# A hybrid RWKV and convolution block: four of seven products side by side through the channels, and half of the weight sums on VectorE

## The chip, the cores and the metric

The kernel runs on one core of one Trainium2 chip. The metric is the device time of one execution in microseconds. Five engines work side by side, each in the order of its own queue: TensorE (PE in the profile, PEld for its weight loads), VectorE (DVE), ScalarE (ACT), GpSimd (POOL) and SyncE (SP), which here only issues DMA transfers. GpSimd issues transfers too, those that add what they bring to what is there.

## The reference, cut to what matters

One layer over 16 meta tokens and 512 tokens of width 2048: a norm, one input projection, a recurrence with a state per head (group A, 1024 channels), a gated convolution (group B, 1024 channels), one output projection, the residual, and a last norm. The change touches the output projection and the little before it:

```python
        y_b = Bg * _causal_depthwise_conv(Cg * hc, conv_w[l]) * jax.nn.silu(g_c)

        mix = jnp.concatenate([y_a, y_b], axis=-1)
        h_res = h_res + mix @ w_out[l]

    out = _rmsnorm(h_res, norm_f_g)
    return out[:, N_META:]
```

`mix` is 512 x 2048, `w_out` 2048 x 2048, all in float32.

## The kernel before

**The input part.** Tiles of 128 columns of the input projection run through TensorE one after the other (`main`, `steps`), from a generator `flow`; the matmuls of the recurrence are put between them. All other work is laid beside this stream. The last tiles are the four of the convolution for channel tile 7: C, h, B, gc. `use` turns the projection of gc into a mix tile `cv` (VectorE, L417), which is written to DRAM (`mixd`, L418) and read back into `mix3` by `split_mix` (L1045), as for all tiles of group B.

**Two parts of a number.** Each float32 operand is split in two parts of TensorE's faster float32 form: ScalarE casts the high part (`hi`, tiles `oh`, `wh`, L1155 and L124), VectorE subtracts it from the whole and gets the low part (`lo`, tiles `ol`, `wl`, L1156 and L125; some low parts of the input projection on GpSimd). A product of two such operands takes three matmuls: high by high, high by low, low by high. `hi` and `lo` have six buffers each; a block of 128 x 1024 weights is two such quarters, so the splits can be three blocks ahead of TensorE. Blocks arrive in `raw`, three buffers.

**The output projection** uses seven products of quarter matrices instead of eight (Strassen's way, in Winograd's form). `mix` is cut in two halves of tokens (T0, T1) and two halves of channels; `w_out` in halves of channels and, for each half of the 2048 output columns (`half` 0 and 1), two column blocks of 512. The left operands are quarters of `mix` or the sums S1, S3, S4, S5 of such quarters, made by `sums` (L1057 to L1060, once for each half `q` of the channel tiles) and split by `split_form` (L1096, L1097). The right operands are weight quarters or sums of them. A weight quarter is four blocks `g` of 256 channels; the block (k, col, g) of a half is `w_out[2 * half + col, 4 * k + g]`, 512 KB.

The products of one half come in this order: M1, M2, M7, Q6, P5, P4, M3, each with its four blocks g in a row. One product with one block is a unit: 12 matmuls of 512 columns (two token tiles s, two quarters, three matmuls; L1184). A product keeps two PSUM banks through its four units and is closed when they are done (`close`): VectorE adds it to the residual rows `xa` (columns 0 to 1023) or `xb` (1024 to 2047) (`onto`, L1165), or to the shared part `sh` (L1206, L1210), which GpSimd then adds to several places (L1207 after Q6, one operation for each s; L1212 after P5, two for each s). ScalarE sums squares of what is complete (`squares`, L1171), GpSimd multiplies by the gain of the last norm (`gain`, L1175).

The right operands of M7, Q6, P5 and P4 are weight sums. They are made by transfer: a block is loaded by SP into a chain tile `x` (M7, L1124), into `spare` or into a `raw` tile `wo` (P5, L1130, L1136), and GpSimd issues a transfer that adds another block to it (`add`, L1145, `accum_op=ALU.add`). Each of these four products has one such accumulation for every block: 16 in a half, 32 in all. M1, M2 and M3 take their blocks straight. The first two blocks of M1 are fetched with the stream of the input weights (`stream += [w_out[0, g] for g in range(2)]`).

`at(u, ...)` and the loop over `units` write down when a load, an accumulation or a split is issued, some units ahead. The order within TensorE is that of the program; on VectorE, ScalarE and GpSimd a scheduler with priorities sets it, up to the last section, where it is written by hand: the last product for the last half (M3 here) is done for token tile 0, then for tile 1 in two parts, while finished rows go out (`finish`, `finish_last`).

Of the kernel before, what the change touches and what calls it, by code (L numbers as in the profile page):

```python
# [18 lines left out]
P = 128  # L19
# [57 lines left out]
def hymba_kernel(ctx: ExitStack, tc: tile.TileContext, xt, xtok, w_in, w_out, pv, lup, cst, msk, gf, out):  # L77
# [39 lines left out]
    stream += [w_out[0, g] for g in range(2)]  # L117
# [257 lines left out]
    def use(what, i, ps):  # L375
# [31 lines left out]
        elif what == "B":  # L407
            cv = got["h", i]
            b = tm(f"b{i}")[:, 0:SEQ]
            scaled(REAL, ps, b, META)  # L410
            nc.gpsimd.tensor_tensor(out=cv, in0=cv, in1=b, op=ALU.mult)
        else:
            cv = got["h", i]
            g = tm(f"gc{i}")[:, 0:SEQ]
            scaled(REAL, ps, g, META)
            gate(g, f"c{i}")
            nc.vector.scalar_tensor_tensor(out=cv, in0=cv, scalar=0.5, in1=g, op0=ALU.mult, op1=ALU.mult)  # L417
            later(9000, lambda: nc.sync.dma_start(mixd[8 + i], cv))  # L418
        ready.add((what, i))

    ready = set()

# [596 lines left out]
    mix = [pp.tile([P, 4, SEQ], F32, tag=f"R{m}", name=f"mix{m}") for m in range(4)]  # L1019
    pt = ExitStack()  # L1020
# [5 lines left out]
    def split_mix(j):  # L1026
# [17 lines left out]
        else:  # L1044
# [30 lines left out]
    for _ in flow:  # L1075
        pass
    sums(1)
# [6 lines left out]
    xa = [pw.tile([P, 1024], F32, name=f"xa{t}") for t in range(4)]  # L1084
# [4 lines left out]
        for f in forms for q in range(2)  # L1089
    }  # L1090

# [11 lines left out]
    slot, right, chain = {}, {}, {}  # L1103
    spare = [None]
# [13 lines left out]
    def request(u):  # L1118
        half, prod, g = units[u]
        if prod in ("M1", "M2", "M3"):  # L1120
            k, c = {"M1": (0, 0), "M2": (1, 0), "M3": (1, 1)}[prod]
        elif prod == "M7":
            slot[u] = chain[g] = pw.tile([P, 1024], F32, tag=f"X{g}", name=f"x{half}{g}")
            nc.sync.dma_start(slot[u], rows_of(half, 0, 1, g))  # L1124
            return
        elif prod == "P5":
            k, c = 0, 0
            if g < 2:
                slot[u] = spare[0][:, 1024 * g : 1024 * g + 1024]
                nc.sync.dma_start(slot[u], rows_of(half, k, c, g))  # L1130
                return
        else:
            slot[u] = chain[g]
            return
        slot[u] = wp.tile([P, 1024], F32, tag="raw", name=f"wo{u}", bufs=3)
        nc.sync.dma_start(slot[u], rows_of(half, k, c, g))  # L1136


    ADDED = {"M7": (1, 1), "Q6": (0, 0), "P5": (0, 1), "P4": (1, 0)}

    def add(u):
        half, prod, g = units[u]
# [4 lines left out]
    def split_unit(u, home=None):  # L1147
        for q in range(2):
            rq = slot[u][:, q * 512 : (q + 1) * 512]
            if home is None:  # L1150
                hi = wp.tile([P, 512], F32R, tag="hi", name=f"oh{u}{q}", bufs=6)
                lo = wp.tile([P, 512], F32R, tag="lo", name=f"ol{u}{q}", bufs=6)
            else:
                hi, lo = home[q]
            nc.scalar.copy(hi, rq)  # L1155
            nc.vector.tensor_tensor(out=lo, in0=rq, in1=hi.bitcast(F32), op=ALU.subtract)  # L1156
            right[u, q] = (hi, lo)
# [9 lines left out]
    def squares(t, n, part=None):  # L1167
        o = slice(0, 512) if part is None else slice(256 * part, 256 * part + 256)
        sq = pw.tile([P, 512], F32, tag="sqj", name=f"sqj{n}_{t}_{part}")
        j = n + (part or 0)  # L1170
# [6 lines left out]
    def product(u, bank, s_):  # L1177
        half, prod, g = units[u]
        for s in s_:
            for q in range(2):  # L1180
                jj = 2 * g + q
                hi, lo = right[u, q]
                for n, (m, w) in enumerate(((0, hi), (0, lo), (1, hi))):
                    nc.tensor.matmul(  # L1184
                        bank[s], left(prod, jj, m, s), w, start=(jj == 0 and n == 0), stop=(jj == 7 and n == 2)
                    )


    def close(half, prod, z):
# [3 lines left out]
        for s in range(2):  # L1193
            d, p = shared[s], z[s]
# [3 lines left out]
            elif prod == "M2":  # L1198
                onto(s, n, p, ALU.add)
                squares(s, n)  # L1200
            elif prod == "M7":
                onto(2 + s, n + 1, p, ALU.subtract)
                onto(2 + s, n, p, ALU.add)
            elif prod == "Q6":
                with ahead():
                    nc.vector.tensor_tensor(out=d, in0=d, in1=p, op=ALU.add)  # L1206
                nc.gpsimd.tensor_tensor(out=here(2 + s, n), in0=here(2 + s, n), in1=d, op=ALU.add)  # L1207
            elif prod == "P5":
                with ahead():
                    nc.vector.tensor_tensor(out=d, in0=d, in1=p, op=ALU.add)  # L1210
                for t in (2 + s, s):
                    nc.gpsimd.tensor_tensor(out=here(t, n + 1), in0=here(t, n + 1), in1=d, op=ALU.subtract)  # L1212
                squares(2 + s, n + 1)
            elif prod == "P4":
                onto(2 + s, n, p, ALU.add)
                squares(2 + s, n)
            else:
                onto(s, n + 1, p, ALU.subtract)
                squares(s, n + 1)

    shared = []
    U = {(half, prod): 28 * half + 4 * PRODUCTS.index(prod) for half in range(2) for prod in PRODUCTS}
# [8 lines left out]
    xb = []  # L1231
# [6 lines left out]
    def load_gain():  # L1238
        t = pp.tile([P, 4, 512], F32, tag="R0", name="gfb").rearrange("p a b -> p (a b)")
        nc.sync.dma_start(t, gf.partition_broadcast(P))  # L1240
        return t

    def load_spare():
        spare[0] = pp.tile([P, 4, 512], F32, tag="R1", name="spare").rearrange("p a b -> p (a b)")

    N_FIRST = 2
    for u, (half, prod, g) in enumerate(units):
        if prod == "M3" and half:
            continue
        if u >= N_FIRST:  # L1250
            early = {"M7": 7, "P5": 5}.get(prod, 3)
            at(u - early, request, u)
            at(u - (4 if prod == "M7" else 3), add, u)
            at(u - 2, split_unit, u)
    for f, (prod, off) in {"S3": ("M1", 0), "S5": ("M2", 0), "S1": ("M7", 0), "S4": ("Q6", 0)}.items():
        for q in range(2):
            at(U[0, prod] + off + 2 * q, split_form, f, q)
    for t in range(4):
        at((-1, 0, 3, 4)[t], load_xa, t)
    at(U[0, "M7"] + 1, load_spare)  # L1260
    at(U[0, "P5"] + 1, lambda: globals_.update(gfb=load_gain()))
    for m in range(2):
        at(U[0, "P4"] + 2 + m, load_xb, m)
    globals_ = {}

    home = []

    def load_home(g):
        u = U[1, "M3"] + g
        request(u)  # L1270
        tiles = [
            pw.tile([P, 4, HT], F32R, tag=f"{f}{g % 2}{a}", name=f"home{g}{a}").rearrange("p a b -> p (a b)")
            for f in (("S3", "S5")[g // 2],) for a in range(2)
        ]
        split_unit(u, [(tiles[0][:, 512 * q : 512 * q + 512], tiles[1][:, 512 * q : 512 * q + 512]) for q in range(2)])

    for g in range(4):
        at(U[1, "P5"] + 1 + 2 * g, load_home, g)

    for q in range(2 * N_FIRST):  # L1280
        j = N_IN + q // 2
        right[q // 2, q % 2] = quarters[2 * j + q % 2]
    for fn, args in calls.pop(-1):
        fn(*args)
    gfb = None
    for u, (half, prod, g) in enumerate(units):
        if half and prod == "M3":
            break
        for fn, args in calls.pop(u, ()):
            fn(*args)  # L1290
        gfb = globals_.get("gfb")
        if g == 0:
            z = [po.tile([P, 512], F32, tag="o", name=f"{prod}{half}{s}") for s in range(2)]
# [143 lines left out]
```

## Time and profile before

| | us |
|---|---|
| median of three runs | 1065.77 (1063.74 to 1068.25) |
| the profiled execution, its time | 1065.86 |
| the profiled execution, its span | 1064.1 |
| granted TensorE clock, mean of the span | 0.984 |
| first matmul of the output projection starts | 860.64 |
| last matmul ends | 1055.23 |

Times in the profile are microseconds from the span's start, where not marked ns. In a group a row reads: line, engine, operation, output<-inputs, shapes and count; then busy time and the mean ns of one; then idle time of the engine before them and what ended most of it. In the table by stretches each engine has its busy time and in brackets its count of instructions; PEclk is the granted clock, the DMA share the mean busy share of the 16 DMA engines. In a table of waits the figures are total, times and longest. In a timeline a row is start, length, engine, line, operation.

### The profile page before, as it was taken

What the parts mean: (1) busy time and instruction counts of PE and PEld (TensorE: products, weight loads), DVE (VectorE), ACT (ScalarE), POOL (GpSimd) and SP (SyncE); (2) the same over time, 40 slices, a digit from 0 to 9 for tenths busy, and PEclk for the clock granted to TensorE, in tenths of its full rate; (3) what the DMA queues carried; (4) which work ended last, traced back from release to release, by engine and by line L of the source; (5) the groups of instructions that cost most, each with busy time, mean ns of one, the idle gap of its engine ahead of it and who ended that gap; (6) DMA issues with size and microseconds to landing.
All of it is one profiled execution on the core that took longest, in us unless ns stands there. A gap on an engine that the chain in (4) does not pass through costs nothing. (4 is left out here: it accounts for less than half of the span.)

```text
span 1064.1 us, 23777 instructions
## 1 busy us (share of the span) xinstructions
PE 1022.3 (96%) x9725; PEld 926.4 (87%) x9725; DVE 664.6 (62%) x1195; ACT 394.4 (37%) x726; POOL 313.2 (29%) x332
## 2 busy tenths in 40 slices
PE   8999999999999999999999999999999998759996
PEld 6999998999989999979999989898898985648875
DVE  6787765668653767653786652354556966567763
ACT  7544322434323444223433232222223353325543
POOL 0132323323222323222232222223323322262333
PEclk9999999999999999999999999999999999889999
DMA  8437386373754375743466649686736869998944
GB/s 293 135 108 167 90 208 184 102 175 106 190 165 126 109 167 119 185 139 103 128 145 164 181 116 329 196 262 182 226 97 178 252 231 291 258 268 243 208 99 159
DMA packets 190077, 188.45 MB, mean 177 GB/s; under 512 B 122128, under 2 KB 144400, under 8 KB 189584
## 3 DMA queue, kind: packets, MB, share of 16 engines
q1 hardware_dynamic: 184784, 169.09, 55.4%
q0 software_dynamic: 4608, 16.78, 8.1%
q8 instruction: 76, 1.25, 0.5%
q10 hardware_dynamic: 576, 1.07, 0.3%
q14 instruction: 33, 0.27, 0.1%
HBM read 150.02 MB, written 36.88 MB: 176 GB/s over the span
## 5 line engine op out<-in xcount | busy, mean ns | idle before, releaser
L125 POOL TENSOR_TENSOR wl<-wr,wh 128x512 fp32r<-128x512 f32 x123 | 171.1, 1391 | 377.0 <-ACT wh L124 354.2
L124 ACT CAST wh<-wr 128x512 fp32r<-128x512 f32 x258 | 156.3, 618 | 311.5 <-PE ps_k L313 52.0
L125 DVE TENSOR_TENSOR wl<-wr,wh 128x512 fp32r<-128x512 f32 x135 | 100.6, 752 | 100.5 <-ACT wh L124 100.0
L313 PE MATMUL ps_k<-xh,wh 128*128 128x264 f32 x256 | 73.3, 286 | 0.0
L313 PE MATMUL ps_k<-xh,wl 128*128 128x264 f32 x256 | 73.2, 286 | 0.0
L313 PE MATMUL ps_v<-xh,wh 128*128 128x264 f32 x256 | 73.1, 286 | 0.0
L313 PE MATMUL ps_k<-xl,wh 128*128 128x264 f32 x256 | 72.9, 285 | 0.0
L313 PE MATMUL ps_h<-xh,wh 128*128 128x258 f32 (+1 forms) x256 | 72.9, 285 | 0.0
L313 PE MATMUL ps_v<-xh,wl 128*128 128x264 f32 x256 | 72.7, 284 | 0.0
L313 PE MATMUL ps_v<-xl,wh 128*128 128x264 f32 x256 | 72.7, 284 | 0.0
L313 PE MATMUL ps_C<-xh,wh 128*128 128x258 f32 (+1 forms) x256 | 72.6, 284 | 0.0
L313 PE MATMUL ps_g<-xl,wh 128*128 128x258 f32 (+1 forms) x256 | 72.4, 283 | 0.0
L313 PE MATMUL ps_h<-xl,wh 128*128 128x258 f32 (+1 forms) x256 | 72.0, 281 | 0.4 <-issue 0.4
L313 PE MATMUL ps_h<-xh,wl 128*128 128x258 f32 (+1 forms) x256 | 72.2, 282 | 0.0
L313 PE MATMUL ps_r<-xh,wh 128*128 128x258 f32 (+1 forms) x256 | 72.1, 282 | 0.0
L313 PE MATMUL ps_r<-xh,wl 128*128 128x258 f32 (+1 forms) x256 | 72.1, 281 | 0.0
L313 PE MATMUL ps_r<-xl,wh 128*128 128x258 f32 (+1 forms) x256 | 72.0, 281 | 0.0
L313 PE MATMUL ps_g<-xh,wh 128*128 128x258 f32 (+1 forms) x256 | 72.0, 281 | 0.0
L313 PE MATMUL ps_C<-xl,wh 128*128 128x258 f32 (+1 forms) x256 | 71.9, 281 | 0.0
L313 PE MATMUL ps_g<-xh,wl 128*128 128x258 f32 (+1 forms) x256 | 71.9, 281 | 0.0
L313 PE MATMUL ps_C<-xh,wl 128*128 128x258 f32 (+1 forms) x256 | 71.9, 281 | 0.0
L1156 DVE TENSOR_TENSOR ol<-x,oh 128x512 fp32r<-128x512 f32 x48 | 43.2, 928 | 31.0 <-ACT oh L1155 30.8
(326 smaller groups left out, 3046.0 us busy)
## 6 DMA issues: line engine op xcount, KB each, us to landing
wr<-in_w_in_dram SPq DMA_DIRECT2D x127, 512.0 KB
ct<-opd SPq DMA_DIRECT2D x64, 288.0 KB
wo<-in_w_out_dram SPq DMA_DIRECT2D x26, 512.0 KB
x<-in_w_out_dram POOLq DMA_DIRECT2D x24, 512.0 KB, 9.4
opd<-ar SPq DMA_DIRECT2D x8, 576.0 KB
opd<-gt SPq DMA_DIRECT2D x16, 288.0 KB
opd<-bt SPq DMA_DIRECT2D x64, 64.0 KB
x<-in_w_out_dram SPq DMA_DIRECT2D x8, 512.0 KB
```

The lines of the kernel that those rows point to most:

```text
L124: nc.scalar.copy(hi, rq)
L125: eng.tensor_tensor(out=lo, in0=rq, in1=hi.bitcast(F32), op=ALU.subtract)
L313: nc.tensor.matmul(ps[r], ww[:, w], xx[:, kt, a:b], start=(kt == 0 and n == 0), stop=(kt == KT - 1 and n == 2))
L1156: nc.vector.tensor_tensor(out=lo, in0=rq, in1=hi.bitcast(F32), op=ALU.subtract)
```

## The change

- The products of a half come in another order: M1; then for each block g the four units P5, M7, M3, Q6; then P4 and M2 mixed, or P4 and then M2 in the second half. The four products side by side hold eight PSUM banks through their 16 units and are closed one after the other behind the last g. M2 takes M3's place as the product of the last section.
- A chain tile `x` holds one growing sum per block g: (0,0), then (0,1) by accumulation (P5's operand), then (1,1) by an addition on VectorE (Q6's), then (1,0) by accumulation (P4's). M7's operand is (0,1) + (1,1), added on VectorE in the tile that holds (0,1). So of the four sums per block two are accumulations (8 in a half, 16 in all) and two are VectorE additions of 128x1024 (L1151 of the new kernel), in place. M3 takes (1,1) straight. In the second half M1's operand is split from the chain tile.
- `spare` is gone; block (0,0) for M1 comes separately in the first half, three blocks of it with the input stream.
- `close`: P5 goes onto both places by VectorE (four additions instead of two), and GpSimd's operations all follow Q6: three for each s.
- The four mix tiles j = 12 to 15 whose gc is still to come when `mix` is allocated (14 and 15) are written by VectorE straight into `mix3`; their way through `mixd` is gone. `sums(1)` stands behind the allocation of the new tiles, and chain tiles are allocated first.
- SP's queue behind the input weights reads now: three prefetched blocks, M1's fourth block, (0,1) and (1,1) of g = 0, chain 0, xa, chain 1, xa, chain 2, (0,1) of g = 1, chain 3, xa twice, xb0, (1,1) of g = 1, and so on. On VectorE the four operations of `sums(1)` and the first split of S1 stand among the splits of M1's fourth block; the addition of M1 onto xa waits for ScalarE's copy of M1, which stands behind the casts of the first P5 block.

```diff
-    stream += [w_out[0, g] for g in range(2)]
+    stream += [w_out[0, g] for g in range(3)]
...
+            o = direct.get(8 + i, cv)
+            nc.vector.scalar_tensor_tensor(out=o, in0=cv, scalar=0.5, in1=g, op0=ALU.mult, op1=ALU.mult)
+            if o is cv:
+                later(9000, lambda: nc.sync.dma_start(mixd[8 + i], cv))
...
-    PRODUCTS = ("M1", "M2", "M7", "Q6", "P5", "P4", "M3")
-    units = [(half, prod, g) for half in range(2) for prod in PRODUCTS for g in range(4)]
+    units = []
+    for half in range(2):
+        units += [(half, "M1", g) for g in range(4)]
+        units += [(half, prod, g) for g in range(4) for prod in ("P5", "M7", "M3", "Q6")]
+        ends = ("P4", 0), ("P4", 1), ("M2", 0), ("P4", 2), ("M2", 1), ("P4", 3), ("M2", 2), ("M2", 3)
+        units += [(half, prod, g) for prod, g in sorted(ends, key=lambda e: half and e[0] == "M2")]
...
-    ADDED = {"M7": (1, 1), "Q6": (0, 0), "P5": (0, 1), "P4": (1, 0)}
-    def add(u):
-        half, prod, g = units[u]
-        if prod in ADDED:
-            k, c = ADDED[prod]
-            nc.gpsimd.dma_start(slot[u], rows_of(half, k, c, g), accum_op=ALU.add)
+    def begin_chain(half, g):
+        if half:
+            chain[g] = new_chain(half, g)
+        nc.sync.dma_start(chain[g], rows_of(half, 0, 0, g))
+    def add_by_transfer(half, k, col, g):
+        nc.gpsimd.dma_start(chain[g], rows_of(half, k, col, g), accum_op=ALU.add)
+    def add(t, *block):
+        x, y = straight[block], t()
+        nc.vector.tensor_tensor(out=y, in0=y, in1=x, op=ALU.add)
...
+            elif prod == "P5":
+                onto(t, n + 1, p, ALU.subtract)
+                onto(s, n + 1, p, ALU.subtract)
...
             elif prod == "Q6":
                 with ahead():
                     nc.vector.tensor_tensor(out=d, in0=d, in1=p, op=ALU.add)
-                nc.gpsimd.tensor_tensor(out=here(2 + s, n), in0=here(2 + s, n), in1=d, op=ALU.add)
-            elif prod == "P5":
-                with ahead():
-                    nc.vector.tensor_tensor(out=d, in0=d, in1=p, op=ALU.add)
-                for t in (2 + s, s):
-                    nc.gpsimd.tensor_tensor(out=here(t, n + 1), in0=here(t, n + 1), in1=d, op=ALU.subtract)
-                squares(2 + s, n + 1)
+                for r, c, op in ((t, n, ALU.add), (t, n + 1, ALU.subtract), (s, n + 1, ALU.subtract)):
+                    nc.gpsimd.tensor_tensor(out=here(r, c), in0=here(r, c), in1=d, op=op)
+                squares(t, n + 1)
+                squares(s, n + 1)
...
+            at(max(o + g, b - 5), add_by_transfer, half, 0, 1, g)
+            at(b - (6 if g else 4), request, half, 0, 1, g)
+            at(b - (4 if g else 3), request, half, 1, 1, g)
+            at(b - 2, split_unit, (half, "P5", g), chained(g))
+            at(b - 1, add, passing(half, 0, 1, g), half, 1, 1, g)
+            at(b - 1, split_unit, (half, "M7", g), passing(half, 0, 1, g))
+            at(b, split_unit, (half, "M3", g), passing(half, 1, 1, g))
+            at(b, add, chained(g), half, 1, 1, g)
+            at(b + 1, split_unit, (half, "Q6", g), chained(g))
+            at(b + 2, add_by_transfer, half, 1, 0, g)
```

Here `b` is the number of the unit (P5, g), and `o` the first unit of the half. The new functions `request` and `split_unit` do what they did, for a named block and unit.

More of the change, by code (lines that the diff above doesn't have):

```diff
@@ L1175, in gain, with product @@
         eng.tensor_tensor(out=h, in0=h, in1=gfb[:, n * 512 : (n + 1) * 512][:, o], op=ALU.mult)
[L1177 to L1178 removed]
+    def product(unit, bank, s_):
+        half, prod, g = unit
         for s in s_:
@@ L1238, in load_gain @@
     def load_gain():
[L1239 to L1254, printed above, removed]
@@ new lines, in load_home, with passing @@
+    def load_home(g):
+        request(1, 1, 0, g)
+        f = ("S1", "S3", "S4", "S5")[g]
+        tiles = [
+            pw.tile([P, 4, HT], F32R, tag=f"{f}0{a}", name=f"home{g}{a}").rearrange("p a b -> p (a b)") for a in range(2)
+        ]
+        split_unit(
+            (1, "M2", g), passing(1, 1, 0, g),
+            [(tiles[0][:, 512 * q : 512 * q + 512], tiles[1][:, 512 * q : 512 * q + 512]) for q in range(2)],
+        )
+    def passing(*block):
+        return lambda: straight[block]
@@ L1277, in hymba_kernel @@
[L1277 to L1282, printed above, removed]
+        at(21 + m, load_xb, m)
+    for n in range(8):
+        at(32 + n, gain, n // 2, n % 2, nc.gpsimd)
+    for t in range(4):
+        at(U[1, "P4", 0] + 1 + t // 2, gain, (2, 3, 0, 1)[t], 3, nc.gpsimd)
+    for e in range(6):
+        right[(0, "M1", e // 2), e % 2] = quarters[2 * N_IN + e]
+    sums(1)
@@ L1283, in hymba_kernel @@
     for fn, args in calls.pop(-1):
         fn(*args)
-    gfb = None
-    for u, (half, prod, g) in enumerate(units):
-        if half and prod == "M3":
+    z = {}
+    for u, unit in enumerate(units):
+        half, prod, g = unit
+        if half and prod == "M2":
             break
```

182 lines of the change are left out of this document (87 added, 95 removed).

## The prediction

> **What bounds the kernel now.** I read the page first, then busy time by stretch of the output projection, then what TensorE (PE) waited for there, then the DMA queues, and last single instructions of VectorE (DVE), ScalarE (ACT) and GpSimd (POOL).
>
> ```profile
> span 1064.1 us, 23777 instructions
> ...
> PE 1022.3 (96%) x9725; PEld 926.4 (87%) x9725; DVE 664.6 (62%) x1195; ACT 394.4 (37%) x726; POOL 313.2 (29%) x332
> ```
>
> ```profile
> core 0: us, PE busy (x) PEld busy (x) DVE busy (x) ACT busy (x) POOL busy (x), PEclk, DMA share, GB/s
> 860.60:873.00 12.40, 12.40 (x54) 9.96 (x54) 9.29 (x13) 8.84 (x14) 0.00 (x0) 1.00 0.67 218
> 873.00:938.00 65.00, 54.61 (x204) 40.04 (x203) 40.98 (x53) 25.57 (x45) 16.84 (x18) 0.92 1.05 283
> 938.00:960.00 22.00, 11.50 (x33) 8.24 (x32) 12.84 (x11) 5.36 (x12) 14.30 (x13) 0.72 1.02 261
> 960.00:1018.00 58.00, 58.00 (x247) 46.60 (x247) 40.87 (x55) 30.90 (x58) 17.62 (x17) 0.99 0.91 228
> 1018.00:1030.00 12.00, 9.44 (x34) 6.94 (x33) 8.89 (x13) 6.02 (x11) 3.33 (x2) 0.86 0.29 75
> 1030.00:1055.30 25.30, 25.22 (x132) 21.30 (x131) 13.22 (x26) 10.16 (x20) 13.59 (x15) 1.00 0.21 79
> ```
>
> TensorE is the bound everywhere else; the share of 96% hides that this stage has holes. The 48 matmuls of 512 columns of the last projection tile give the undisturbed pitch; the chain gives the last 48 of 256 columns and the end.
>
> ```profile
> 849.52 0.40 PE L313 MATMUL ps_gc<-xh,wh 128*128 128x512 f32 x1
> ...
> 860.64 0.40 PE L1184 MATMUL M<-wh,m 128*128 128x512 f32 x1
> ```
>
> ```profile
> 1049.47 5.76 PE end L1368 x48
> 1055.23 0.02 issue
> ```
>
> (860.64 - 849.52) / 48 = 0.2317 us, so 2.78 us for a unit of 12. The stage has 52 units and 24 more wide matmuls: 648 x 0.2317 + 5.76 = 155.9 us. It takes 1055.23 - 860.64 = 194.6, so **38.7 us are lost**. By stretch (length less matmuls times pitch): 17.7 in 873 to 938, 14.4 in 938 to 960, 4.1 in 1018 to 1030, little elsewhere. Part of this is a lower granted clock after each hole (1.00 in the last, 0.72 in the third row), not waiting. After the last matmul come 1064.1 - 1055.23 = 8.9 us.
>
> ```profile
> PE P L1184 <- DVE ol L1156: 12.9, 5, 5.8
> PE Q L1184 <- ACT oh L1155: 5.6, 2, 5.3
> ...
> ACT oh L1155 <- DMA x<-in_w_out_dram: 21.7, 8, 7.7
> ```
>
> ```profile
> q1 hardware_dynamic: 9923, 31.44, 40.0%
> q0 software_dynamic: 4608, 16.78, 38.4%
> ```
>
> TensorE waits for split weights, their splits wait for the accumulating transfers, and the DMA engines are full (1.05, 1.02) in just the two bad stretches. The queues are of 840 to 1064 us: 224 x 0.384 / 32 = 2.7 us of all engines for an accumulating block, 224 x 0.400 / 31.44 x 0.524 = 1.5 us for a plain one.
>
> **The change part by part.** *Transfers.* Accumulating blocks fall from 32 to 16, plain weight blocks from 40 to 36: 16 x 2.7 + 4 x 1.5 = 49 us less DMA work. A half then needs some 18 x 1.5 + 8 x 2.7 = 49 us (the first half 15 more, for ten such blocks of residual and gain) beside 28 x 2.78 = 78 us of matmuls. I let the 17.7 us of the first stretch go, and in the second what POOL's late queue caused (about 7). Not all blocks are fetched once: (0,1) and (1,0) still come straight and by accumulation. Dropping the mixd round trip for two tiles gains nothing: TensorE did not wait for it. If the engines stayed as full as before, 17.7 us would come back.
>
> *VectorE* gets 16 sums of 128x1024 and four more additions onto the output.
>
> ```profile
> L1156 DVE TENSOR_TENSOR ol<-x,oh 128x512 fp32r<-128x512 f32 x48 | 43.2, 928 | 31.0 <-ACT oh L1155 30.8
> ...
> L1155 ACT CAST oh<-x 128x512 fp32r<-128x512 f32 x48 | 28.3, 617 | 42.3 <-DMA x<-in_w_out_dram 21.7 <-PE M L1184 12.5 <-PE Q L1184 2.2
> ...
> L1097 DVE TENSOR_TENSOR S<-mix,S 128x1024 fp32r<-128x1024 f32 x8 | 9.8, 1222 | 0.5 <-ACT S L1096 0.5
> ...
> L1165 DVE TENSOR_TENSOR xa<-xa,M 128x512 f32<-128x512 f32 x10 | 6.6, 683 | 0.1
> ```
>
> 16 x 1.22 + 4 x 0.68 = 22 us more. In steady state a group of four units costs 8 x 0.69 + 2 x 1.22 = 8.0 us of DVE beside 11.1 of TensorE, so it hides; without that cover it would cost its full 22. ACT has the same casts as before, 8 x 0.62 = 5 us in 11.1. POOL loses 16 transfers to issue and keeps its 24 operations on tiles.
>
> *The start.* Here the new order costs. sums(1), four operations of 1.22, and the first split of S1 now stand in DVE's queue among the splits of M1's fourth block. And the first P5 block needs a chain that a load and an accumulation build.
>
> ```profile
> 860.67 0.62 ACT L1155 CAST oh<-wo 128x512 fp32r<-128x512 f32 x1 [2.21 <-PE ps_gc L313]
> ```
>
> ```profile
> 855.86 1.29 POOL L125 TENSOR_TENSOR wl<-wr,wh 128x512 fp32r<-128x512 f32 x1 [0.48 <-ACT wh L124]
> ```
>
> ```profile
> 863.04 0.69 DVE L417 SCALAR_TENSOR_TENSOR cv<-cv,gc 128x512 f32<-128x512 f32 x1
> ```
>
> ```profile
> 866.81 0.33 SPq L1045 DMA_DIRECT2D mix<-mixd  x1
> ```
>
> ```profile
> 871.40 0.62 ACT L1046 CAST m<-mix 128x512 fp32r<-128x512 f32 x1 [1.23 <-DMA mix<-mixd]
> ```
>
> ```profile
> DMA to landing us min/median/max: 6.3/9.4/14.9
> ```
>
> The last mix tile is whole at 863.7; copy 0.62, lo 0.69, then sums, S1 and two lo parts (4 x 1.22 + 2 x 0.69): M1's last lo part is there at 871.3, wanted at 869.7, so 1.6 us. Beside this runs the chain: SP's load of it stands behind a load whose buffer is free only when POOL has split the third prefetched block. That split's cast waits for the last gc block (860.67), plus 0.62 and 1.29: 862.6; two issues: 863.3. A load took 4.6 us from issue to reader (866.81 to 871.40), so 867.8, and the accumulation 6.3 to 14.9. I take 8, between least and median, as the queues are full only to about 876: t = 875.8. From below, ACT's queue has two casts that wait for sums(1) ahead, so t is not under 873.9. From t on: two casts 1.23, the copy of M1 0.6 (it stands behind them, and DVE's addition onto xa behind it), 0.68, 0.69: P5 begins at t + 3.2. Then 0.68, 0.69, S4 1.22, sum 1.22, S5 1.22, lo 0.69 before M7's block: t + 8.9 = 884.7, where an unbroken stream would be at 860.64 + 5 x 2.78 = 874.5. **The start costs 10 us** (8 to 17), and some 2 of low clock behind a hole of 6.
>
> *Queues moved past.* On SP the load of xb0, 1 MB, now stands ahead of the second group's block (1,1) and waits until S4 has been split off mix2, about 882 by the line above; two loads of 4.6 put the block at 891, just when its sum is due, so nothing to 2 us, and I take nothing. On POOL the second half's first accumulation stands behind six gain products of the first half, the last two of which need P4 closed (unit 25); P5 reads the chain in unit 32. The six units between are 17 us, and 3 us of products, 9.4 of landing and 2 of splits fit in. If they did not, each us of lateness would be one of TensorE's.
>
> *The closes.* P5, M7, M3 and Q6 now end together, and six POOL operations follow Q6 at a stretch, with four gain products behind them, where two and four were apart. POOL and DVE lock each other out:
>
> ```profile
> 949.34 6.30 DVE L1156 TENSOR_TENSOR ol<-x,oh 128x512 fp32r<-128x512 f32 x1 [3.62 <-ACT oh L1155]
> ```
>
> ```profile
> 953.18 1.89 POOL L1175 TENSOR_TENSOR xa<-xa,gfb 128x512 f32<-128x512 f32 x1
> ```
>
> ```profile
> 1032.26 1.29 POOL L1212 TENSOR_TENSOR xb<-xb,sh 128x512 f32<-128x512 f32 x1 [6.44 <-DVE sh L1210]
> ```
>
> ```profile
> 1032.78 1.32 DVE L1156 TENSOR_TENSOR ol<-x,oh 128x512 fp32r<-128x512 f32 x1 [0.60 <-ACT oh L1155]
> ```
>
> At 949.34 a split of 0.69 stood until POOL's last gain product ended at 955.07; at 1032.78 one got in after a single POOL operation. POOL's run after the change begins from a wait, as at 1032, so I take that row: each lo part waits for one operation, 1.29 + 0.69 = 2.0 us, two to a unit, against 2.78. Ten POOL operations slow four to five units: 4 x 1.0 = **4 us at the first close**; at the second, home splits stand among the lo parts, so ten operations of 2.0 must pass where TensorE has the last of them due some 12 us on: **8 us**, with 1 of low clock in all.
>
> The Trainium skill, page "SBUF — State Buffer", section "Who interferes with whom", speaks against the change here: a DVE instruction with two SBUF inputs and a GpSimd one that reads SBUF exclude each other, the second blocking until the first has finished. By that rule a wait is one operation, as at 1032; the trace also shows several, so the rule alone would give my sum, and the 6.30 row a worse one. Its page "DMA: Bandwidth & Descriptors", "Anatomy of one DMA — SWDGE (gpsimd) path", fits 2.0 us plus bytes / 436 GB/s, an estimate of 3.2 us for 512 KB; the trace's least is 6.3. With 3.2 the start would cost 8 rather than 10.
>
> *Sum*: 10 + 2 + 4 + 8 + 1 = 25 us lost instead of 38.7. TensorE ends at 860.64 + 155.9 + 25 = 1041.5, the span at 1050.4. The profiled run took 1065.86, 1.8 more than its span, and the median is 1065.77, 0.1 under it: **1052 us**.
>
> **The rivals.** *The lock costs next to nothing* (0.15): the lo parts are three units ahead when Q6 closes, as the six buffers allow. Loss 8 + 2 + 2 + 2 = 14: 1041. Against it: DVE must add ten products to the output just then.
>
> *Starved closes* (0.25): as at 949.34, DVE gets in only when POOL's run ends. Ten operations of 1.29 hold it 12.9 us; with the lo part that follows and less the one unit at hand, 12.9 + 0.7 - 2.8 = 10.8 at each close. With 12 at the start and 3 of low clock behind two holes 36.6 us are lost: 1064, no change that counts. For it: 6.30 us is the worst split of the trace. Against it: POOL's run there followed straight on a transfer that POOL issued, and behind Q6 it will not.
>
> *Slower* (0.12): the same place and lock, but with the mean duration that POOL's gain products have in this stage, 1.63 us:
>
> ```profile
> L1175 POOL TENSOR_TENSOR xa<-xa,gfb 128x512 f32<-128x512 f32 x8 | 11.6, 1630 | 7.1 <-ACT sqj_None L1171 7.1
> ```
>
> Ten hold DVE 16.3 us, and TensorE stands 16.3 + 0.7 - 2.8 = 14.2 at each close; with 12 at the start and 4 of low clock 44.4 us are lost, 5.7 more than now: 1072. It turns from gain to loss at 1.35 us an operation, where a close costs 11.3. The forecast itself has 0.43.
>
> *It does not do what it says* (0.05): half of the sums leave the transfers but stand between the splits on DVE, with a cast on ACT behind each, and the lead of three units does not cover them; the 22 us of added DVE work then all show, on top of the forecast: 1074. Against it: 8.0 us of 11.1 leave room.
>
> **How the numbers follow.** About 0.5% (5.3 us) is what a measurement of this kernel can tell. Faster by more: all of the forecast and of the first rival, and of the starved case the half whose start is short: 0.43 + 0.15 + 0.12 = 0.70. Slower: 0.12 and some of the last case: 0.14. Same: 0.16. The range takes both ends of the start and the starved case: 1040 to 1068.
>
> **What would show it.** Right: an accumulation count of 16, DMA share under 1.0 beyond 880; no TensorE wait for splits between the eighth unit and the first close; one hole of 4 to 7 us near 873 to 880; lo parts of 1.3 to 2 us beside POOL's runs. Wrong: a full DMA later than 890, or no hole at the start (then the gain is larger), or lo parts of 6 us and more behind POOL's runs (then it is gone).

## The result, and the profile after

The changed kernel takes **1053.88 us** (median of 4 runs, 1051.41 to 1055.72) beside 1065.99 for the kernel before (4 runs, 1063.74 to 1068.25): a ratio of 0.9885, 95% interval 0.9852 to 0.9918, so 12 us faster. 1052 was predicted. The profiled execution is the longest of the four, 1055.72.

From the page of the kernel after, the span and the engines:

```profile
span 1053.9 us, 23740 instructions
...
PE 1020.1 (97%) x9725; PEld 925.4 (88%) x9725; DVE 684.0 (65%) x1214; ACT 394.3 (37%) x726; POOL 306.8 (29%) x317
```

VectorE (DVE) has 19 us more than before (664.6) and GpSimd (POOL) 6 less. TensorE's (PE) timeline of after gives the first matmul of the output projection and its stops of half a microsecond and more; the chain gives the last 48 matmuls and the end:

```profile
863.90 0.40 PE L1190 MATMUL M<-wh,m 128*128 128x512 f32 x1
...
874.57 0.50 PE L1190 MATMUL M<-ol,m 128*128 128x512 f32 x1 [0.78 <-DVE ol L1162]
...
880.82 0.79 PE L1190 MATMUL P<-oh,S 128*128 128x512 f32 x1 [4.11 <-ACT oh L1161]
883.15 0.80 PE L1190 MATMUL P<-ol,S 128*128 128x512 f32 x1 [1.54 <-DVE ol L1162]
...
888.59 0.50 PE L1190 MATMUL M<-ol,S 128*128 128x512 f32 x1 [0.53 <-DVE ol L1162]
...
1012.10 0.49 PE L1190 MATMUL Q<-ol,S 128*128 128x512 f32 x1 [2.92 <-DVE ol L1162]
...
1021.48 0.50 PE L1190 MATMUL P<-ol,m 128*128 128x512 f32 x1 [0.72 <-DVE ol L1162]
...
1026.53 0.62 PE L1190 MATMUL P<-ol,m 128*128 128x512 f32 x1 [2.68 <-DVE ol L1162]
```

```profile
1039.53 5.76 PE end L1391 x48
1045.31 0.43 DVE xb L1395
```

The stage takes 1045.31 - 863.90 = 181.4 us; less the undisturbed 155.9 it loses 25.5, where before it lost 38.7. The stage begins 3.3 us later than before (860.64), and this has nothing to do with its own order. The busy times of 640 to 660 us, first of before, then of after, and the one wait that only after has in 590 to 720:

```profile
640.00:660.00 20.00, 19.87 (x262) 19.11 (x261) 3.35 (x6) 4.84 (x9) 3.83 (x3) 1.00 0.91 327
```

```profile
640.00:660.00 20.00, 18.74 (x193) 17.79 (x193) 2.66 (x5) 4.24 (x8) 3.68 (x3) 0.91 0.83 299
```

```profile
PE rz L903 <- DMA ct<-opd: 1.3, 3, 0.4
```

A wait of 1.3 us and the lower clock behind it (0.91) come from code that the change doesn't touch. In the kernels below, which have the same code there, the stage begins between 858.3 and 861.7. So a profiled run's whole time can carry some 5 us that the edit did not make, and below each edit is read from the loss inside the stage, and from the time only where the interval allows it.

Busy time by stretch of after (the columns are those of the prediction's table), cut in the hole of the start (877.8) and at the first matmul of the second group, of the first P4, of the second half's first group, of its last Q6 unit and of M2:

```profile
863.90:877.80 13.90, 11.90 (x49) 8.67 (x47) 11.16 (x12) 8.61 (x11) 3.25 (x3) 1.00 0.79 251
877.80:896.90 19.10, 14.02 (x49) 10.24 (x50) 13.82 (x18) 8.37 (x14) 2.63 (x3) 0.82 1.05 322
896.90:930.50 33.60, 33.60 (x146) 27.03 (x145) 30.81 (x44) 15.70 (x27) 3.02 (x4) 1.00 0.73 200
930.50:966.80 36.30, 34.92 (x146) 26.58 (x145) 31.17 (x32) 19.36 (x42) 25.35 (x18) 1.00 0.64 168
966.80:1008.80 42.00, 42.00 (x182) 33.78 (x180) 31.50 (x47) 21.70 (x38) 2.63 (x3) 1.00 0.65 167
1008.80:1033.90 25.10, 18.28 (x62) 12.86 (x61) 22.53 (x26) 7.25 (x17) 17.29 (x11) 0.86 0.13 22
1033.90:1045.30 11.40, 11.38 (x73) 10.19 (x71) 4.81 (x12) 5.44 (x11) 4.67 (x9) 1.00 0.45 172
```

Where PE's first column equals the length, nothing is lost: in the third and fifth rows, the side-by-side groups of both halves. The losses sit in the start, the first close (fourth row) and the second close (sixth).

To compare kernels, the loss up to a unit is the start of its first matmul, less the first of the stage, less 12 x 0.2317 for each unit ahead of it (the undisturbed unit here is 2.80, so 0.02 a unit is no loss but the pitch). The parts of the stage, in us, read in this way from PE's timeline of each profiled execution:

| kernel | start (M1 to M3 of g0) | second group | to the first P4 | first close (P4, M2, next M1) | second half's groups, to its last Q6 | last Q6 unit | second half's P4 | all |
|---|---|---|---|---|---|---|---|---|
| after | 10.7 | 0.1 | 0.2 | 3.0 | 0.3 | 4.6 | 6.6 | 25.4 |
| s1: sums(1) late | 7.8 | 1.3 | 0.6 | 3.4 | 0.3 | 4.3 | 7.7 | 25.2 |
| s2: first P5 sum on DVE | 9.5 | 1.9 | 0.2 | 3.0 | 0.3 | 4.5 | 6.5 | 25.7 |
| s3: both | 3.1 | 5.2 | 0.2 | 2.6 | 0.3 | 2.0 | 7.4 | 20.6 |
| s4: closing additions on DVE | 10.9 | 0.1 | 0.2 | 0.9 | 0.3 | 1.4 | 2.5 | 16.2 |
| s6: sums twice | 14.2 | 0.6 | 3.7 | 4.6 | 0.3 | 5.2 | 8.6 | 37.2 |
| s7: second gains on DVE | 10.7 | 0.1 | 0.2 | 3.4 | 0.3 | 5.0 | 4.1 | 23.7 |
| s8: joined | 3.2 | 4.6 | 0.2 | 0.9 | 0.3 | 2.3 | 2.5 | 13.8 |
| s9: loads held back | 3.2 | 1.7 | 0.2 | 1.0 | 0.3 | 3.3 | 4.1 | 13.8 |
| s10: additions deferred | 4.6 | 1.5 | 1.2 | 0.4 | 0.3 | 5.9 | 0.3 | 14.4 |
| s11: both | 3.2 | 1.7 | 0.2 | 0.6 | 0.3 | 5.7 | 0.2 | 11.8 |
| s12: last Q6 first | 4.9 | 0.1 | 0.2 | 0.4 | 0.3 | 0.0 | 2.7 | 8.5 |

Each row is one execution, and its parts scatter. In after, s1, s2 and s3 every engine has the same order of work in the second half; yet they lose 2.0 to 4.6 in the last Q6 unit and 6.5 to 7.7 in P4. s11 and s12 have the same order in the start and lose 3.2 and 4.9 there. So a difference of 2 to 3 us between two rows is not by itself the effect of an edit.

### The profile page after: what moved, and what is told of

Its sections match the earlier page's. It is cut to its first block, busy times and chain, and to the rows that moved or that the text cites. A ratio compares the mean times of both kernels' runs of the same rounds, so it can differ in the third digit from the quotient of the medians.

```text
span 1053.9 us, 23740 instructions
## 1 busy us (share of the span) xinstructions
PE 1020.1 (97%) x9725; PEld 925.4 (88%) x9725; DVE 684.0 (65%) x1214; ACT 394.3 (37%) x726; POOL 306.8 (29%) x317
## 5 line engine op out<-in xcount | busy, mean ns | idle before, releaser
L313 PE MATMUL ps_gc<-xh,wl 128*128 128x512 f32 x128 | 51.1, 399 | 0.9 <-DVE wl L125 0.9
```

What stands on the lines that cost most here:

```text
L313: nc.tensor.matmul(ps[r], ww[:, w], xx[:, kt, a:b], start=(kt == 0 and n == 0), stop=(kt == KT - 1 and n == 2))
```

## The experiments

**The start (s1, s2, s3).** Three kernels, each the changed one with one edit or both. s1 moves sums(1) behind the first splits, since its four operations feed only the S forms of tiles 4 to 7, which group 2 needs:

```diff
-    sums(1)
     for fn, args in calls.pop(-1):
...
+    at(5, sums, 1)
```

> The changed kernel with the four operations of sums(1) moved from ahead of the product stage to the sixth unit; the first chain is still built by an accumulating transfer. Theory (the chain's 8 us of landing sets the start): P5 still begins near 880.8 for a first matmul at 863.9, only what follows it is quicker (the copy of M1 and S4 no longer stand behind sums(1)), so the loss at the start falls from 10.3 to 7 or 8 us and the time by 2 to 3. Rival (the order on VectorE sets the start): the loss falls to 2 us or less and the time by 8.

s2 adds the first P5 sum on DVE:

```diff
-            at(max(o + g, b - 5), add_by_transfer, half, 0, 1, g)
+            if half or g:
+                at(max(o + g, b - 5), add_by_transfer, half, 0, 1, g)
             at(b - (6 if g else 4), request, half, 0, 1, g)
+            if not (half or g):
+                at(1, add, chained(0), 0, 0, 1, 0)
```

> The changed kernel with the first block's P5 sum added on VectorE instead of by an accumulating transfer; sums(1) stays ahead. Theory (the chain's landing sets the start, and behind it the order on VectorE and ScalarE is late by nearly as much): the sum is there at 872 instead of 880, but the second lo part waits behind the copy of M1, which stands behind five casts of sums: P5's second lo part near 882 instead of 883.8; the loss at the start falls from 10.3 to 7 to 9 us. If the transfer were the only cause, the loss would fall to 2 us and the time by 8.

s3 has both edits.

> Both edits of the start together: sums(1) in the sixth unit, the first block's P5 sum on VectorE. If the two cover each other, the loss at the start falls from 10.3 to 1 to 3 us, more than the two single gains added, and the time by 7 to 9 (about 1045). If the copy of M1 on ScalarE or the load of the third block is next, 5 us stay.

Measured: 1049.17 us for s1 (0.9798 to 0.9862 of before), 1051.01 for s2 (0.9829 to 0.9885), 1047.98 for s3 (0.98 to 0.9856). The start loses 7.8, 9.5 and 3.1 instead of 10.7: s1 as its first theory has it, s2 0.5 and s3 0.1 above theirs. The gains are 2.9 and 1.2 alone (the 1.2 is within the scatter) and 7.6 together. Two things are late by nearly as much, the accumulated chain and the queue of sums(1), and neither shows in full until the other is gone. The whole stage tells another story: s1 and s2 have given back all of their gain by its end (25.2 and 25.7 lost), and s3 most of what it saved in the start: its second group now loses 5.2. Of the 4.8 us by which s3's stage is shorter, 2.5 lie in the start and the second group; 2.6 lie in the last Q6 unit, which the edit does not touch. In the profiled executions s1 and s2 are ahead mainly because the stage began earlier (859.02 and 860.91); where their other executions gain is not shown.

What is next in s3 stands in SyncE's (SP) and DVE's timelines:

```profile
877.36 0.47 SPq L1245 DMA_DIRECT2D gfb<-in_gf_dram  x1
879.36 0.33 SPq L1142 DMA_DIRECT2D wo<-in_w_out_dram  x1
```

```profile
888.10 1.23 DVE L1151 TENSOR_TENSOR wo<-wo,wo 128x1024 f32<-128x1024 f32 x1 [1.85 <-DMA wo<-in_w_out_dram]
```

The block (1,1) of the second group is issued at 879.36, behind 1 MB of gain vector, and is there for DVE at 888.10, 8.7 us later, where the prediction's row had 4.6.

**The closes (s4, s7).** s4 moves the six closing additions behind Q6 from POOL to DVE, in both halves:

```diff
-                    nc.gpsimd.tensor_tensor(out=here(r, c), in0=here(r, c), in1=d, op=op)
+                    nc.vector.tensor_tensor(out=here(r, c), in0=here(r, c), in1=d, op=op)
```

> The changed kernel with the six closing additions behind Q6 on VectorE instead of GpSimd in both halves (24 operations fewer for the lock to act in: 12 of 22 GpSimd operations of the closes; 12 x 0.69 us more of VectorE work). Theory (each GpSimd operation holds a lo part until it ends): the loss at the second close falls from 12 to about 5 us (the four gain products stay on GpSimd), the first close stays at 2 to 3, and the time falls by 6 to 8 to about 1046. Rival (VectorE is simply full at the close): 4.1 us of added work at each close make it longer, the second close loses 14 to 16 and the time rises by 3 or more.

(The count in the brackets is loose: 12 operations move, 6 at each close.) Measured: 1043.59 us, ratio 0.9793 (0.9761 to 0.9824); the second close loses 3.9 instead of 11.2, the first 0.9 instead of 3.0. The theory's 5 us for the second close was 1 too high, and the first close gains too. The rival is out: with 8 us more work on DVE both closes are shorter. But of the 7.3 us at the second close only the 4.1 in P4 (6.6 to 2.5) can be put down to the additions. The splits of the last Q6 unit run before any of them, since they wait for Q6 to close, and this unit's 1.4 instead of 4.6 is near the 2.0 that s3 has without the edit.

s7 moves only the four gain products of the second close:

```diff
-        at(U[1, "P4", 0] + 1 + t // 2, gain, (2, 3, 0, 1)[t], 3, nc.gpsimd)
+        at(U[1, "P4", 0] + 1 + t // 2, gain, (2, 3, 0, 1)[t], 3, nc.vector)
```

> The changed kernel with the four gain products of the second close (column 3) on VectorE instead of GpSimd; the six closing additions stay on GpSimd. Theory (the lock's price goes by the number of GpSimd operations): of the 11.2 us of the second close four tenths go, so 6.5 to 8 stay; the first close is unchanged at 2.5. Rival (the price is all in the six additions, which stand right behind Q6): the second close stays at 10 or more.

Measured: 1050.03 us (0.9806 to 0.9891). The second close loses 9.1: neither the 6.5 to 8 of the theory nor the 10 of the rival. In P4 alone, whose splits stand beside these operations, the four products are worth 2.5 us (6.6 to 4.1) and the six additions 4.1, so 0.6 to 0.7 us each: by number, as the theory has it. What it had wrong is the last Q6 unit, whose loss (5.0 here) it counted among the lock's. The two prices do not add: with both moved (s8, below) P4 loses 2.5, as with the additions alone.

**Half the sums on DVE in the old order (s5).** The kernel before, with the second block of M7's and P5's sums loaded straight and added on DVE; 16 accumulating transfers become plain ones, and nothing is fetched less often:

```diff
-        if prod in ADDED:
+        if prod in ("M7", "P5"):
+            t = wp.tile([P, 1024], F32, tag="raw", name=f"ws{u}", bufs=3)
+            nc.sync.dma_start(t, rows_of(half, *ADDED[prod], g))
+            nc.vector.tensor_tensor(out=slot[u], in0=slot[u], in1=t, op=ALU.add)
+        elif prod in ADDED:
```

> The kernel before, in its old order of products, with only the sums of M7 and P5 changed: their second block is loaded straight and added on VectorE (16 additions of 128x1024), so that 16 of the 32 accumulating transfers become plain ones; no block is fetched less often. Theory (the accumulating transfers filled the DMA engines and held the splits): 16 x (2.7 - 1.5) = 19 us less transfer work, and the loss of the stage falls from 38.7 to 25 to 30 us. Rival (the order and the fetches are what counts): the loss stays at 36 or more.

Measured: 1057.32 us (median of 8, 0.9883 to 0.9945 of before), 32.7 us lost in the stage: 5.9 less than before on the same measure (38.6), between theory and rival. Its DMA queues of 840 to 1059 us:

```profile
q1 hardware_dynamic: 12577, 40.59, 54.6%
q0 software_dynamic: 2304, 8.39, 19.7%
```

219 x (0.546 + 0.197) = 163 us of all engines, where before had 224 x 0.784 = 176 and after (rows below) 214 x 0.612 = 131. So somewhat less than half of the 13.2 us that the change gains inside the stage is had by the DVE sums alone. By the times of all runs it is more, 9 of 12 us, with 6 to 12 in the interval of s5. The rest, by subtraction, falls to the order with its blocks fetched once, which carries the dear start and closes with it; how large it is stays open between these two readings.

**The sums twice (s6).** Behind each DVE sum an operation of the same shape that leaves it as it is:

```diff
         nc.vector.tensor_tensor(out=y, in0=y, in1=x, op=ALU.add)
+        nc.vector.tensor_tensor(out=y, in0=y, in1=y, op=ALU.max)
```

> The changed kernel with every weight sum on VectorE followed by a second operation of the same shape on the sum, which leaves it as it is: 16 more of 128x1024, 20 us of VectorE work. Theory (VectorE has 8.0 us of work to 11.1 of TensorE in a group, so its sums are hidden): the loss stays within 25 to 28 us, what is added lies at the start, where the first M7 sum is waited for. Rival (the sums stand between the splits and show): 15 us or more on top, 40 lost.

Measured: 1064.38 us (median of 10, 0.9944 to 0.9993), 37.2 us lost: 11.8 of the 20 added show, which is nearer to the rival than to the theory. The two stretches of groups, first half and second:

```profile
897.50:935.00 37.50, 34.50 (x145) 26.66 (x144) 37.05 (x50) 15.07 (x27) 2.82 (x4) 1.00 0.60 151
973.00:1015.00 42.00, 42.00 (x182) 33.79 (x181) 38.37 (x52) 19.88 (x36) 2.64 (x3) 1.00 0.69 166
```

In the second half DVE works 38.4 of 42 us and PE loses nothing: there the sums are hidden, twice over. In the first half DVE is busy 37.05 of 37.5 and PE loses 3.7 up to the first P4: the splits of the S forms for tiles 4 to 7 stand there too. Start and closes, where DVE's order is the path, pay the rest.

**The edits joined (s8), and what is left (s9 to s12).** s8 has s3's and s4's edits, the second gains on DVE, and the gain vector in the memory of mix tile 1 ("R1" for "R0"), which comes free later.

> The edits joined: sums(1) in the sixth unit, the first P5 sum on VectorE, the six closing additions and the second close's gains on VectorE, and the gain vector loaded into the memory of mix tile 1, which comes free later than that of mix tile 0, so that its 1 MB stands behind the second group's weights. Theory: the start loses 1 to 3 us, the second group 0 to 3, the first close 1, the second 1 to 2: 4 to 8 us lost instead of 25, and a time of 1030 to 1037. Rival (the DMA engines are full up to 905 and hold the second group whatever the order): 5 us stay there, and the time is 1038 or more.

Measured: 1042.4 us (0.973 to 0.9821), 13.8 lost. The start (3.2) and the first close (0.9) are near the theory's; the second close loses 4.8 where it had 1 to 2, and the second group 4.6, as the rival has it. That the order does not matter is not shown by this, for with the gain vector moved SyncE issues xb0, as large, ahead of the second group's block:

```profile
878.16 0.48 SPq L1241 DMA_DIRECT2D xb<-in_xtok_dram  x1
880.16 0.33 SPq L1142 DMA_DIRECT2D wo<-in_w_out_dram  x1
```

So in s9 the loads of xa2, xa3, xb0, xb1 and gfb wait for one column that DVE copies from a lo part of group 2 or 3 into their memory:

```diff
+    def behind(t, unit):
+        nc.vector.tensor_copy(t, right[unit, 1][1][:, 0:1].bitcast(F32))
...
+        if t > 1:
+            behind(xa[t][:, 0:1], (0, "P5", 2))
```

> The joined kernel, with the loads of the residual and of the gain vector (xa2, xa3, xb0, xb1, gfb: 4 MB) each held behind one lo part of groups 2 and 3 by a copy of one column into their memory. Theory (the DMA engines are full up to 905 because these loads stand beside the first groups' weights, and with the start short the second group pays for it): the 4.8 us that the second group loses fall to 1.5 or less, and the stage loses 10 to 11 instead of 13.7. Rival (the chains' loads and accumulations fill the engines by themselves): 4 us or more stay.

In s10 the closing additions follow the splits of P4, and the second gains are back on POOL; s11 has both edits:

```diff
-                for r, c, op in ((t, n, ALU.add), (t, n + 1, ALU.subtract), (s, n + 1, ALU.subtract)):
-                    nc.vector.tensor_tensor(out=here(r, c), in0=here(r, c), in1=d, op=op)
...
+                at(U[half, "P4", 2], closing, s, d, n)
```

> The joined kernel, with the six closing additions put on VectorE behind the splits of P4 instead of ahead of them, and the second close's gains back on GpSimd, behind the same splits. Theory (what is left at the second close is VectorE's queue, 9 operations onto the output and 6 additions of 0.6 us between the splits): of 4.8 us lost there 1.5 to 3 stay. Rival (gains on GpSimd hold the home splits as in the changed kernel): 4 us or more stay.

> Both edits on the joined kernel: by the two theories 7 to 9 us lost in the stage and a time of 1035 to 1038; by the rivals 12 or more and 1041.

Measured: 1040.09 us (0.9707 to 0.9789), 1040.2 (0.9692 to 0.9789) and 1037.98 (0.9689 to 0.9763). The second group loses 1.7 in s9 and s11, near the theory's 1.5. But s9's stage as a whole loses 13.8, no less than s8's: its second close, where VectorE has the same order as in s8, loses 7.4 instead of 4.8. s11 loses 11.8, near the rivals' 12 and not the theories' 7 to 9; that its time is the theories' is no proof of them, as its stage began at 858.3. The busy times of 885 to 900 us in s8 and in s9 show what was freed (the last three columns are clock, DMA share and GB/s):

```profile
885.00:900.00 15.00, 12.62 (x46) 9.50 (x45) 13.72 (x18) 5.42 (x9) 0.88 (x1) 0.89 0.97 306
```

```profile
885.00:900.00 15.00, 13.97 (x60) 10.70 (x59) 15.00 (x19) 6.47 (x10) 1.03 (x2) 1.00 0.64 164
```

But s10, which holds no load back and has s8's order of work there, also loses only 1.5, behind a start that is 1.4 longer. Start and second group together are 4.9 in s9, s11 (and 5.0 in s12), 6.1 in s10, 7.8 and 8.3 in s8 and s3; that the held loads are the whole cause is likely and not settled.

At the second close neither theory held. s10 takes P4's loss away (0.3), yet the unit ahead, the last Q6, loses 5.9, and its total stays above 4, as the rival had it though not by the rival's cause: POOL computes nothing beside these splits. PE's only wait at that close, and DVE's timeline of s11:

```profile
PE Q L1190 <- DVE ol L1162: 4.0, 1, 4.0
```

```profile
991.35 0.69 DVE L1162 TENSOR_TENSOR home<-wo,home 128x512 fp32r<-128x512 f32 x1 [2.27 <-ACT home L1161]
991.96 2.48 DVE L1171 TENSOR_TENSOR xb<-xb,P 128x512 f32<-128x512 f32 x4
994.35 3.07 DVE L1171 TENSOR_TENSOR xb<-xb,M 128x512 f32<-128x512 f32 x5
997.34 0.69 DVE L1162 TENSOR_TENSOR home<-wo,home 128x512 fp32r<-128x512 f32 x1
997.94 0.68 DVE L1171 TENSOR_TENSOR xb<-xb,M 128x512 f32<-128x512 f32 x1
998.54 2.49 DVE L1162 TENSOR_TENSOR ol<-x,oh 128x512 fp32r<-128x512 f32 x4
```

Ten additions onto the output, which run with high priority, and the last of which waits for M3 to close, stand ahead of the lo parts of the last Q6. They begin behind a split of M2's weights (`home`), for which DVE has stood idle for 2.27 us. s12 gives that unit's sum and splits a higher priority still:

```diff
+    def early(fn, *args):
+        with tc.high_priority(offset=3 * AHEAD):
+            fn(*args)
...
+            if half and g == 3:
+                at(b, early, split_unit, (half, "Q6", g), chained(g))
```

> The kernel of the run before (loads held back, closing additions deferred), with the sum and the splits of the last Q6 unit put ahead of the ten additions of P5, M7 and M3 onto the output on VectorE. Theory (what is left at the second close is no lock of GpSimd but VectorE's queue: the lo parts of the last Q6 unit stand behind ten additions of 0.6 us, and one of these waits for M3 to close, a unit before Q6 is due): the 5.7 us that this unit loses fall to 1.5 or less, the stage loses 6 to 8 instead of 11.7, and the time is 1031 to 1035. Rival (VectorE has too much to do there in any order): what Q6 gains is lost in P4, 10 or more stay lost.

Measured: 1036.88 us (median of 5, 0.9697 to 0.9752 of before); the last Q6 unit loses 0.0 instead of 5.7, P4 2.7, the stage 8.5. The loss is 0.5 above the theory's range and the time 2; the last Q6 unit's 5.7 us were the queue. The rival has a part in it: 2.5 of the 5.7 come back in P4 (0.2 to 2.7). s12 is 30 us faster than before (1067.03 in the same runs) and, by the two ratios (0.9725 and 0.9885), 17 faster than the changed kernel; beside s11 its time is the same within the scatter.

## Why the prediction was right, point by point

**The total was right, two of its terms were off in opposite directions.** Predicted: 25 us lost, PE's end at 1041.5. Measured: 25.5 lost and 1045.31, of which 3.26 is the later begin of the stage. That the loss comes within 0.5 is in part luck, as the terms below show.

**Transfers: right in amount, wrong in one sign.** The DMA queues of 840 to 1054 us of after, and from the accumulated tiles' view the landing times of the transfers (minimum, median, maximum):

```profile
q1 hardware_dynamic: 9178, 29.17, 39.2%
q0 software_dynamic: 2304, 8.39, 22.0%
```

```profile
DMA to landing us min/median/max: 5.4/7.4/9.6
```

16 accumulating transfers remain and 176 - 131 = 45 us of DMA work are gone (49 predicted). But the DMA share did not fall under 1.0 beyond 880: from 877.8 to 896.9 it is 1.05, in the table above, and 890 to 905 has 1.01:

```profile
890.00:905.00 15.00, 15.00 (x66) 12.06 (x65) 13.86 (x18) 6.55 (x12) 1.12 (x2) 1.00 1.01 318
```

The text named this as a sign that it was wrong, and the sign was badly chosen. The working summed a whole half (49 + 15 us of transfers beside 78 of matmuls), while all of the residual's loads are issued in the first 40 us. PE did not pay, because after the hole of the start the blocks were there in time (0.1 lost in the second group). s3 shows the price as soon as that hole is taken away: 5.2 us. For the same reason the step that took 1 MB ahead of the second group's block as nothing held only under the cover of the start.

**The start: right (12 with the clock predicted, 10.7 measured), and by its mechanism.** SP, POOL, ACT and DVE of after, one answer each:

```profile
866.37 0.38 SPq L1138 DMA_DIRECT2D x<-in_w_out_dram  x1
```

```profile
871.09 1.08 POOL L1147 DMA_DIRECT2D x<-in_w_out_dram  x1 [5.17 <-DMA x<-in_w_out_dram]
```

```profile
880.15 1.14 ACT L1161 CAST oh<-x 128x512 fp32r<-128x512 f32 x2 [5.49 <-DMA x<-in_w_out_dram]
```

```profile
881.80 0.69 DVE L1171 TENSOR_TENSOR xa<-xa,M 128x512 f32<-128x512 f32 x1 [5.01 <-ACT sh L1204]
```

Shifted by the 3.26 us, M1's last lo part was expected at 874.6, and PE's wait for it ends at 874.57. The load was expected to be issued at 866.6 and there at 871.1, the sum at 879.1, P5's lo part at 882.3 and M7's at 888.0; the rows have 866.37, 871.09, 880.15, 883.15 (PE's wait) and 888.59. As predicted, the addition of M1 onto xa waits for the copy that stands behind the casts, and the lo part behind it. The step had the second lateness in it: the sum not before 873.9 on account of sums(1), 1.9 us ahead of the 875.8 taken. So undoing the chain alone could bring little; it brought 1.2 in s2, and s1 to s3 show the second lateness under the first.

**DVE hidden: right as far as it was asked.** 31.50 us of 42.00 in the fifth row of the stretches is 8.4 to a group of 11.2; 8.0 of 11.1 was predicted. The rival "all sums show" is out for the change itself. s6 limits it: the cover is real in the second half, used up in the first.

**The closes: two terms mis-sized.** Predicted 4 and 8 with 1 of clock; measured 3.0 and 11.2. The lock's form was right. One round of it at the second close, DVE's and POOL's rows, and the range of all lo parts of accumulated tiles (minimum, median, maximum in ns):

```profile
1019.66 1.77 DVE L1162 TENSOR_TENSOR ol<-x,oh 128x512 fp32r<-128x512 f32 x1
```

```profile
1019.15 1.73 POOL L1218 TENSOR_TENSOR xb<-xb,sh 128x512 f32<-128x512 f32 x1
1020.84 1.73 POOL L1218 TENSOR_TENSOR xb<-xb,sh 128x512 f32<-128x512 f32 x1
```

```profile
L1162 DVE TENSOR_TENSOR ol<-x,oh x56: 677/690/1781, 882.4 to 1029.8; 128x512 fp32r<-128x512 f32 x56
```

The split at 1019.66 ends at 1021.43, 0.6 us after POOL's operation from 1019.15 gave way at about 1020.8; then POOL's next one waits in its turn. A lo part costs 1.77 us, the longest takes 1.78, and 1.3 to 2 was said. So the starved case (6 us and more) did not come, nor the slower one, though POOL's additions and gain products do last 1.58 to 1.72 us in the means of their groups: from 1.35 on the prediction had the gain turn into a loss if DVE had to wait for all of them in a row. It waits for one at a time. The rule of the Trainium skill, page "SBUF — State Buffer", section "Who interferes with whom", by which the second of the two blocks until the first has finished, agrees with 1.77 us as one operation's wait.

The failed step is the second close's 8 us: the sum put all of it on the lock. The lock's part, in P4, is some 6: after loses 6.6 there, and s10, where the same splits run with nothing on POOL beside them, 0.3. The other 4.6 us lie a unit earlier. There PE has waited 2.92 us (with a lower clock behind it) before POOL's first operation, and the wait is DVE's queue: ten additions onto the output ahead of the last Q6 unit's lo parts, as s11 and s12 show. How long the wait gets depends on when these additions can begin, behind a split of M2's weights, and so on the landing of a load; that is where the 2.0 to 4.6 of kernels with one order come from, as far as the traces tell. The prediction saw these additions only as an argument against its first rival and gave them no price. With 1.3 us too much at the start and 1 at the first close, against 2.2 too little at the second (9 with its clock), the sum came out all the same; that is luck.

**The landing.** For 512 KB the Trainium skill, page "DMA: Bandwidth & Descriptors", section "Anatomy of one DMA — SWDGE (gpsimd) path", gives an estimate of 3.2 us; the least here is 5.4, and the row was the right choice. The first chain's took some 9, from 871.09 to 880.15 above, where 8 was taken.

## What to carry to other kernels

When two chains are late by almost the same, undoing either shows next to nothing; undo both before calling one harmless, and then look at once for the resource that the hole had covered (here the DMA engines, full for 20 us while nobody waited for them). At a place where several products close together, count the high-priority additions on the evacuating engine as a queue ahead of the next split, apart from any lock between engines. And a whole-run time that scatters by 5 us ahead of the stage is no judge of an edit worth 2: compare the stage's own loss, part by part, and take from kernels that are alike in a part how far that part scatters.

## What was not expected of the hardware

The lock between DVE and POOL is taken in turns in one place and not in another. At after's second close the two alternate, 1.77 and 1.73 us each. In s4, where DVE has ten operations in a row without a wait, POOL's first gain product stands beside them for 5.13 us and DVE's splits run at full speed:

```profile
1012.82 5.13 POOL L1249 TENSOR_TENSOR xb<-xb,gfb 128x512 f32<-128x512 f32 x1 [6.78 <-ACT sqj_None L1177]
```

```profile
1014.31 2.49 DVE L1162 TENSOR_TENSOR ol<-x,oh 128x512 fp32r<-128x512 f32 x4
```

Before, at 949.34, it was DVE that stood for 6.30 us. Which of the two a place gets is open; no run here decides it.
